# Loads, constants and one tile's projection moved across the phase borders of layer 0 in a two-layer latent-token backbone

## The chip, the cores and the metric

The kernel runs on one NeuronCore of a Trainium2 chip. The metric is the device time of one execution in microseconds (us), median of three runs. In the rows, PE is TensorE (PEld its weight loads), DVE VectorE, ACT ScalarE, POOL GpSimd, SP SyncE, which issues all DMAs of this kernel (SPq is its queue). PEclk is the clock granted to TensorE as a share of full speed.

## What is computed

Two layers over 256 context tokens and 2048 latent tokens of width 1024, in fp32. Layer 0 is the part that matters here. From normalized rows `h` one wide projection gives `u, v, ga, q, k, vv, gb`; two heads groups use it, and one output projection joins them:

```python
u, v, ga, q, k, vv, gb = _split(h @ w_in, AB_SIZES)
ya = chunk_gmlp(gelu(u), gelu(v), ln_g, ln_b, w_s, b_s) * silu(ga)   # group norm of v, then
                                   # u * (w_s @ v + b_s) in chunks of 128 tokens, 4 groups
yb = window_attention(q, k, vv, kc, vvc, sink) * silu(gb)            # +-128 tokens and context
y  = concatenate([ya, yb]) @ w_out
x  = x + gate * y
```

Layer 1 is a gated linear recurrence in both directions (`r, ig = sigmoid(z @ w + b)`, `a = exp(-8 * r * softplus(-lam))`, a scan per direction), followed by a last normalization. Its convolution weights, biases and `softplus(-lam)` are constants which the kernel prepares during layer 0.

## The kernel before

A tile is 128 tokens: 2 context and 16 latent tiles, `t` from 0 to 17, 9 pairs. fp32 products are made from two fp32r parts (high and low): each block is three matmuls, lines 91, 92 and 93 (`mm3`), with 128x512 results for a tile's projection on 512 columns, 8 blocks, 24 matmuls.

Layer 0 has three phases, each with its own pools of SBUF and PSUM. A pool of a later phase takes the memory that an earlier one gave back, and each of its tiles waits for the last users of the place.

**Attention** (to about 658 us). For every tile: normalized rows are transposed, split and spilled to DRAM (`h0s`), `q` and `k`, `vv` are projected, and scores (`pc`, `pl`), softmax, transposes (`ptp`), values (`po`, line 574) and the output (`os`) follow for units of two heads, some steps behind. The program merges these lists by fractions, and a scheduler orders each engine's instructions by priority and modelled readiness. Into attention fillers are put which need only `h`: `ga` of tiles 2 to 17 and, in its last three steps, a queue `tail_q` with `ga` of tiles 0 and 1 and the values `v` of the tiles in `V_TILES` (`pu`, written to `gv`). `TAIL` says how much of the queue each quarter step takes. Low-priority work (`FILL`) prepares layer 1's weights (`keep_halves`, `whl`, `kept`).

**Mixing** (to about 854 us; pools `a2b1`, `a2b2`). For each tile: rows are loaded (`load_h`, line 778, three buffers), `v` comes from `gv` or is projected (`pvv`), gelu and group norm give `vhl`, `u` is projected (`pu`), and per pair the 128x128 mixing (`sv`), the scale and bias and the transposes (`yatp`) give `ya`, written to `yas`. `consts()` is called after tile 0's values: it loads and transposes `w_s` (`wstp`), loads 92 rows of constants (`cr`), transposes them (`cvtp`) and computes the softplus. The sixth unit of weights for `u` is split at the beginning of the phase (ScalarE the high part, GpSimd the low parts).

**Gates and output** (pools `a3b1`, `a3b2`). `gate_b(pr)` loads the attention output of a pair (`ot`) and its rows (`hp3`, line 919, one buffer), projects the gate (`pg`, 96 matmuls of 128x256) and gives `ybT`; `out_a(t)` multiplies with `w_out` (`po`: blocks 0 to 3 with `yaT`, 4 to 7 with `ybT`, two halves, 48 matmuls).

Weights live in pools `wa` (3 buffers), `wb0` (2) and `wb` (1), used in turn. SyncE issues in order: a DMA that waits for its buffer holds all behind it.

Of the kernel before, what the change touches and what calls it, by code (L numbers as in the profile page):

```python
# [15 lines left out]
P = 128  # L16
D = 1024
KT = D // P
# [10 lines left out]
GA_FROM = 2  # L29
FILL = 400  # L30
WG_AT = (3, 5, 7, 9)
V_TILES = (3, 5, 7, 9, 11, 13, 15)
TAIL = (0, 4, 8, 12, 16, 20, 24, 28, 32, 38, 44, 50, 56)
U_AT = 5
T_PE = 14
BACK = 13
LAG = 4
MOD_AT = 8
# [4 lines left out]
def backbone_kernel(ctx: ExitStack, tc: tile.TileContext, a, out):  # L43
# [221 lines left out]
    with ExitStack() as c1:  # L265
# [375 lines left out]
        for i, (_, mm) in enumerate(tail):  # L641
            tail_q += mm
            if i + 2 < len(tail):
                tail_q.append(tail[i + 2][0])
            if i == U_AT:
                tail_q += wu_halves(wa, 4)
        n_tail = [len(tail_q) * f // TAIL[-1] for f in TAIL]

        def mod_bank():
# [70 lines left out]

    w_out0 = a["ab_w_out"][0]


    with ExitStack() as c2:
        b1 = c2.enter_context(tc.tile_pool(name="a2b1", bufs=1, reuse_waits="tile"))
# [2 lines left out]
        lng = bc_row(b1, a["a_ln_g"][0], "lng", 512)  # L728
        lnb = bc_row(b1, a["a_ln_b"][0], "lnb", 512)

        def consts():
            wsr = raws.tile([P, 4, P], F32, tag="raw", name="wsr")
            sp.dma_start(wsr, a["a_w_s"][0].rearrange("g p q -> p g q"))
            wsT = b1.tile([P, 2, 4, P], F32R, name="wsT")
            tp = bank([P, 4, P], "wstp", "t")
            for g in range(4):
                pe.transpose(tp[:, g], wsr[:, g], ident)
            split(wsT[:, 0], wsT[:, 1], tp)
            cr = raws.tile([92, P], F32, tag="raw", name="cr")
            r0 = 0  # L740
            for src in (a["c_conv_w"][0].rearrange("k (c p) -> (k c) p", p=P), a["c_conv_b"][0].rearrange("(c p) -> c p", p=P),
                        a["c_b_a"][0].rearrange("k (c p) -> (k c) p", p=P), a["c_b_i"][0].rearrange("k (c p) -> (k c) p", p=P),
                        a["c_lam"][0].rearrange("k (c p) -> (k c) p", p=P), a["a_b_s"][0]):
                n = src.shape[0]
                sp.dma_start(cr[r0:r0 + n], src)
                r0 += n
            tpc = bank([P, 92], "cvtp", "t")
            pe.transpose(tpc, cr, ident[0:92, 0:92])
            dve.tensor_copy(cv[:, 0:92], tpc)
            bs = cv[:, 88:92]  # L750

            def softplus_neg(pool_):
                t = [pool_.tile([P, 16], F32, name=f"spt{i}") for i in range(4)]
                dve.tensor_scalar(t[0], lam, -1.0, None, ALU.mult)
                dve.tensor_tensor(t[1], t[0], lam, ALU.min)
                act.activation(t[1], t[1], AF.Exp)
                dve.tensor_scalar(t[2], t[1], 2.0, None, ALU.add)
                dve.reciprocal(t[2], t[2])
                dve.tensor_tensor(t[1], t[1], t[2], ALU.mult)
                dve.tensor_tensor(t[2], t[1], t[1], ALU.mult)  # L760
                dve.memset(t[3], 2.0 / 19.0)
                for i in range(8, -1, -1):
                    dve.tensor_tensor(t[3], t[3], t[2], ALU.mult)
                    dve.tensor_scalar(t[3], t[3], 2.0 / (2 * i + 1), None, ALU.add)
                dve.tensor_tensor(t[3], t[3], t[1], ALU.mult)
                dve.tensor_scalar(t[0], t[0], 0.0, None, ALU.max)
                dve.tensor_tensor(sps[:, 0], t[0], t[3], ALU.add)
                dve.tensor_scalar(sps[:, 1], sps[:, 0], 4.0, None, ALU.mult)
                dve.tensor_scalar(sps[:, 2], sps[:, 0], -8.0, None, ALU.mult)

            softplus_neg(b1)
            return wsT, bs

        ubs, vhls, hps, ths = {}, {}, {}, {}

# [67 lines left out]
                act.activation(yT[:, x], tp, AF.Copy)  # L843
            sp.dma_start(yas[pr].rearrange("p x (g c) -> p x g c", c=P), yT)

        with tc.high_priority():
            load_h(0)
        load_h(1)
        wu = wus + [unit_w(wu_cols(5), act, (pool, pool))]
        part_g(0)  # L850
        wg, wo, halves = [], [], []
# [18 lines left out]
        for t in range(NT - 2):  # L870
            load_h(t + 2)
            if t:
                part_g(t)
            part_v(t)
            if t == 0:
                wsT, bs = consts()
            if t in WG_AT:
                halves.pop(0)()
            if t in WO1_AT:
                with tc.high_priority(offset=-FILL):  # L880
                    ahead.pop(0)()
            part_u(t)
            if t % 2 == 0 and t:
                pair_b(t // 2 - 1)
# [20 lines left out]
    with ExitStack() as c3:  # L905
# [7 lines left out]
        def gate_b(pr):  # L913
            ot = b2.tile([P, 2, 4, P], F32, tag="ot", name="ot")
            for x in range(2):
                sp.dma_start(ot[:, x], os_[2 * pr + x])
            hp = b1.tile([P, 2, 2, KT, P], F32R, tag="hp3", name="hp3")
            for x in range(2):
                sp.dma_start(hp[:, x].bitcast(F32), h0s[2 * pr + x])
            ybT = b2.tile([P, 2, 4, 2, P], F32R, tag="ybT", name="ybT")  # L920
            for half in range(2):
                pg = bank4([P, 2, 2, P], "pg")
                for cc in range(2):
                    for k in range(KT):
                        mm3(pg[:, cc], lambda hl: wg[half][:, hl, k, cc * P:(cc + 1) * P],
                            lambda hl: hp[:, :, hl, k], k == 0, k == KT - 1)
                sg = b2.tile([P, 2, 2, P], F32, tag="sg", name="sg")
                act.activation(sg, pg, AF.Silu)
                dve.tensor_tensor(sg, sg, ot[:, :, 2 * half:2 * half + 2].rearrange("p t c q -> p c t q"), ALU.mult)
                c = slice(2 * half, 2 * half + 2)  # L930
                split(ybT[:, 0, c], ybT[:, 1, c], sg)
            return ybT
# [54 lines left out]
        for pr in range(NPAIR):  # L987
# [4 lines left out]
            for x in range(2):  # L992
                if pr == NPAIR - 1 and x == 0:
                    op0 = next_w().tile([P, KT, 2, 2, P], F32R, tag="w", name="op0")
                    sp.dma_start(op0.bitcast(F32), h1s[0])
                    wx = [unit_w(w_in1[:, 0:U], act, (dve, dve))]
                if pr == NPAIR - 1 and x == 1:
                    ahead = []
                    for i in range(2, 2 + N_AHEAD):
                        ahead.append(raws.tile([P, 4, U], F32, tag="raw", name="raw"))  # L1000
                        unit, half = divmod(i, 2)
                        src = w_in1[512 * half:512 * half + 512, U * unit:U * (unit + 1)]
                        sp.dma_start(ahead[-1], src.rearrange("(k p) c -> p k c", p=P))
                f = out_a(2 * pr + x, yaT, ybT)
                if pend:
                    pend()
                pend = f
                for n in [1] if (pr, x) == (0, 0) else [pr + 2] if x else []:
                    if n < NPAIR:
                        gated.append(gate_b(n))  # L1010


    L = NPAIR
# [519 lines left out]
```

## Time and profile before

| | |
|---|---|
| median of 3 runs | 1976.6 us (1975.62 to 1977.08) |
| profiled execution | 1978.54 us |
| its span, first to last instruction | 1976.8 us |
| mean granted clock of TensorE | 0.982 |
| busy: PE, DVE, ACT, POOL | 1879.1, 1450.0, 1060.8, 564.7 us |
| moved by DMA | 371 MB, 188 GB/s on average |

All rows below are from that one execution, with times from the start of its span. A row of a timeline gives start, duration, engine, line, operation, what is written and read, how many, and in brackets the idle time of the engine before it and what ended it. A row of waits gives the engine, what it was about to run, whom it waited for, total us, times and the longest.

### The profile page before, as it was taken

What the parts mean: (1) busy time and instruction counts of PE and PEld (TensorE: products, weight loads), DVE (VectorE), ACT (ScalarE), POOL (GpSimd) and SP (SyncE); (2) the same over time, 40 slices, a digit from 0 to 9 for tenths busy, and PEclk for the clock granted to TensorE, in tenths of its full rate; (3) what the DMA queues carried; (4) which work ended last, traced back from release to release, by engine and by line L of the source; (5) the groups of instructions that cost most, each with busy time, mean ns of one, the idle gap of its engine ahead of it and who ended that gap; (6) DMA issues with size and microseconds to landing.
All of it is one profiled execution on the core that took longest, in us unless ns stands there. A gap on an engine that the chain in (4) does not pass through costs nothing. (4 is left out here: it accounts for less than half of the span.)

```text
span 1976.8 us, 28764 instructions
## 1 busy us (share of the span) xinstructions
PE 1879.1 (95%) x9919; PEld 1577.9 (80%) x9919; DVE 1450.0 (73%) x2943; ACT 1060.8 (54%) x1965; POOL 564.7 (29%) x769
## 2 busy tenths in 40 slices
PE   7999999999999799979999999999999999899898
PEld 3778878888888688868888887888888877687677
DVE  7888989786755787636777842498989656978873
ACT  6656656675745443324544551376656666666542
POOL 2755555564422211210000000144421221312211
PEclk8999999999999899989999999999999999999999
DMA  9355443552345689366565664334535736955643
GB/s 351 126 176 179 156 171 118 178 175 91 129 134 171 205 328 354 131 245 226 188 242 193 230 203 159 112 123 155 179 134 178 239 140 229 322 194 175 201 152 123
DMA packets 174398, 371.28 MB, mean 188 GB/s; under 512 B 18566, under 2 KB 72586, under 8 KB 166060
## 3 DMA queue, kind: packets, MB, share of 16 engines
q1 hardware_dynamic: 174252, 369.44, 53.6%
q8 instruction: 78, 1.28, 0.3%
q14 instruction: 68, 0.56, 0.1%
HBM read 242.22 MB, written 127.17 MB: 187 GB/s over the span
## 5 line engine op out<-in xcount | busy, mean ns | idle before, releaser
L91 PE MATMUL px<-op,w 128*128 128x512 f32 (+1 forms) x576 | 220.4, 383 | 10.1 <-DMA op<-h1s 9.9
L92 PE MATMUL px<-op,w 128*128 128x512 f32 (+1 forms) x576 | 218.4, 379 | 0.0
L93 PE MATMUL px<-op,w 128*128 128x512 f32 (+1 forms) x576 | 218.4, 379 | 0.0
L544 POOL TENSOR_SCALAR s<-s,ri 128x640 f32<-128x640 f32 (+2 forms) x144 | 133.9, 943 | 96.6 <-DVE ri L541 92.6
L536 ACT ACTIVATE s<-s,mn 128x641 f32<-128x641 f32 (+2 forms) x144 | 113.4, 788 | 65.9 <-DVE mn L518 58.8
L85 ACT ACTIVATE pT<-ptp 128x512 fp32r<-128x512 f32 (+1 forms) x192 | 99.6, 535 | 90.7 <-PE ptp L562 87.6
L88 DVE TENSOR_TENSOR zhl<-zf,zhl 128x512 fp32r<-128x512 f32 x72 | 57.3, 805 | 115.0 <-ACT zhl L85 114.8
L91 PEld LDWEIGHTS px<-op,w 128*128 128x128 f32 x576 | 109.0, 189 | 36.4 <-DMA op<-h1s 16.8
L574 PE MATMUL po<-pT,v 128*128 128x256 f32 x656 | 130.5, 297 | 6.8 <-DVE pT L88 4.4
L1127 POOL TENSOR_TENSOR ig<-ig,zf 128x512 f32<-128x512 f32 x72 | 104.9, 1462 | 102.0 <-ACT ig L1125 91.1
L88 DVE TENSOR_TENSOR pT<-ptp,pT 128x512 fp32r<-128x512 f32 (+1 forms) x192 | 114.3, 604 | 23.5 <-ACT pT L85 22.9
L93 PEld LDWEIGHTS px<-op,w 128*128 128x128 f32 x576 | 108.9, 189 | 20.4
L92 PEld LDWEIGHTS px<-op,w 128*128 128x128 f32 x576 | 109.1, 189 | 19.7
L1170 POOL COPY carry<-T 128x1 f32<-128x1 f32 x60 | 47.9, 802 | 259.1 <-DVE T L1168 256.8
L902 DVE STREAM_TRANSPOSE h1T<-hrow 32x256 f32<-32x256 f32 x224 | 97.7, 436 | 31.1 <-ACT hrow L954 28.1
L92 PE MATMUL px<-w,op 128*128 128x512 f32 x256 | 103.0, 402 | 14.9 <-DVE op L88 14.9
L574 PEld LDWEIGHTS po<-pT,v 128*128 128x128 f32 x656 | 98.9, 189 | 17.8 <-DVE pT L88 9.0
L164 POOL TENSOR_SCALAR ms<-ss 128x1 f32<-128x1 f32 x36 | 10.1, 280 | 353.0 <-ACT junk L162 346.0
L562 PE MATMUL ptp<-ident,s 128*128 128x128 f32 x656 | 104.7, 274 | 3.9 <-POOL s L544 2.1
L91 PE MATMUL px<-w,op 128*128 128x512 f32 x256 | 102.2, 399 | 4.0 <-DVE xt L1276 4.0
L93 PE MATMUL px<-w,op 128*128 128x512 f32 x256 | 102.3, 400 | 0.0
L518 DVE CUSTOM_DVE_ANT_0 s<-pl,mask,mn 128x384 f32<-128x384 f32 (+1 forms) x128 | 76.0, 594 | 32.8 <-PE pl L516 31.4
(279 smaller groups left out, 5804.4 us busy)
## 6 DMA issues: line engine op xcount, KB each, us to landing
hp<-h0s SPq DMA_DIRECT2D x45, 1024.0 KB
op<-h1s SPq DMA_DIRECT2D x56, 512.0 KB
mraw<-in_w_mod SPq DMA_DIRECT2D x48, 512.0 KB
h0s<-hT SPq DMA_DIRECT2D x18, 1024.0 KB
h1s<-h1hl SPq DMA_DIRECT2D x36, 512.0 KB
xt<-in_x SPq DMA_DIRECT2D x32, 512.0 KB
gs<-gs SPq DMA_DIRECT2D x64, 256.0 KB
raw<-in_ab_w_in SPq DMA_DIRECT2D x22, 512.0 KB
```

Of the source, the lines that this page charges most:

```text
L85: act.activation(hi, src, AF.Copy)
L88: (eng_lo or dve).tensor_tensor(lo, src, hi.bitcast(F32), ALU.subtract)
L91: pe.matmul(ps, lhsT=lhs(0), rhs=rhs(0), start=first, stop=False)
L92: pe.matmul(ps, lhsT=lhs(1), rhs=rhs(0), start=False, stop=False)
L93: pe.matmul(ps, lhsT=lhs(0), rhs=rhs(1), start=False, stop=last)
L518: dve.tensor_tensor_reduce(out=s[:, 1 + 2 * P:1 + 2 * P + n_l], in0=pl[:, 0:n_l], in1=mask[:, 2 * P + off:2 * P + off + n_l], scale=-1.0, ...
L536: act.activation(s[:, 0:nk], s[:, 0:nk], AF.Exp, scale=-1.0, bias=st["mn"][:, row, i:i + 1], accum_out=st["sm"][:, i:i + 1])
L544: pool.tensor_scalar(s[:, 1:nk], s[:, 1:nk], ri[:, i:i + 1], 0.0, ALU.mult, ALU.add)
L562: pe.transpose(tp[:, x, h], s_t[h][:, 1 + i * P:1 + (i + 1) * P], ident)
L574: pe.matmul(pos[t, g][:, 2 * P * e:2 * P * (e + 1)], lhsT=vl, rhs=pT[:, hl, x], start=i == 0 and hl == 0, stop=i == n - 1 and hl == 1)
L902: dve.transpose(out[o, :, s], src[s, :, o])
L1127: pool.tensor_tensor(res[1], res[1], zfs.pop((d, i, b)), ALU.mult)
```

## The change

- `load_hp01` loads the rows of tiles 0 and 1 into one buffer of `wb0`, from two thirds of the tail's queue on; mixing takes them from there and no longer calls `load_h` for them.
- Tile 1 joins `V_TILES`: its `v` is projected in the tail, and read back in mixing.
- `consts()` becomes `spatial()`, called after tile 1's values, and `columns()`, at low priority after tile 4's. The mixing's bias `bs` gets a tile and a load of its own, four elements per partition straight from DRAM, and `cr` has 88 rows.
- `hp3` moves to a pool `gaterows`, opened before mixing; pair 0's rows are loaded at tile 12 of mixing (as the program is written).

```diff
-V_TILES = (3, 5, 7, 9, 11, 13, 15)
+V_TILES = (3, 5, 7, 9, 11, 13, 15, 1)
...
+HP3_AT = 12
...
+        hp01 = []
+
+        def load_hp01():
+            hp01.append(wb0.tile([P, 2, 2, KT, P], F32R, tag="w", name="hp01"))
+            for t in range(2):
+                sp.dma_start(hp01[0][:, t].bitcast(F32), h0s[t])
+
+        tail_q.insert(len(tail_q) * 2 // 3, load_hp01)
         n_tail = [len(tail_q) * f // TAIL[-1] for f in TAIL]
...
+    mid = ctx.enter_context(ExitStack())
+    gaterows = mid.enter_context(tc.tile_pool(name="gaterows", bufs=1, reuse_waits="tile"))
+
+    def load_pair(pr):
+        hp = gaterows.tile([P, 2, 2, KT, P], F32R, tag="hp3", name="hp3")
+        for x in range(2):
+            sp.dma_start(hp[:, x].bitcast(F32), h0s[2 * pr + x])
+        return hp
...
-        def consts():
+        wsT = b1.tile([P, 2, 4, P], F32R, name="wsT")
+        bs = b1.tile([P, 4], F32, name="bs")
+        sp.dma_start(bs, a["a_b_s"][0].rearrange("g p -> p g"))
+
+        def spatial():
...
+        def columns():
+            cr = raws.tile([88, P], F32, tag="raw", name="cr")
...
-        with tc.high_priority():
-            load_h(0)
-        load_h(1)
+        for t in range(2):
+            hps[t] = hp01[0][:, t]
...
-            if t == 0:
-                wsT, bs = consts()
+            if t == 1:
+                spatial()
+            if t == 4:
+                with tc.high_priority(offset=-FILL):
+                    columns()
...
+            if t == HP3_AT:
+                hp3 = [load_pair(0)]
...
-            hp = b1.tile([P, 2, 2, KT, P], F32R, tag="hp3", name="hp3")
-            for x in range(2):
-                sp.dma_start(hp[:, x].bitcast(F32), h0s[2 * pr + x])
+            hp = hp3.pop() if hp3 else load_pair(pr)
```

What stands in a row on an engine is set by the scheduler. From attention to mixing, TensorE before (`po` ends attention, `pvv` is tile 0's first projection in mixing; the brackets name the semaphores waited for):

```order
L574 MATMUL po<-pT,v 128x256 [waits DVE_49]
L574 MATMUL po<-pT,v 128x256 x2
L737 MATMUL wstp<-ident,wsr 128x128 [waits DMAHW3_49,DVE_49]
L737 MATMUL wstp<-ident,wsr 128x128 x3
L748 MATMUL cvtp<-ident,cr 128x92 [waits DMAHW4_49,DMAHW5_49,DMAHW1_49,DMAHW6_49,DMAHW0_49,DMAHW7_49,DVE_49,PE_49]
L91 MATMUL pvv<-w,hp 128x512 [waits DMAHW5_49]
L92 MATMUL pvv<-w,hp 128x512
L93 MATMUL pvv<-w,hp 128x512
```

The same place of TensorE after the change (lines of the changed file, one higher here; `hp_8190` is the buffer filled by `load_hp01`):

```order
L575 MATMUL po<-pT,v 128x256 [waits DVE_49]
L575 MATMUL po<-pT,v 128x256 x2
L92 MATMUL pvv<-w,hp_8190 128x512
L93 MATMUL pvv<-w,hp_8190 128x512
L94 MATMUL pvv<-w,hp_8190 128x512
```

The transposes of `w_s` moved behind 37 matmuls of tile 0, those of the constants to the middle of mixing, and `pvv` has no wait. In the tail, 15 of tile 1's 24 matmuls stand in one block behind tile 15's and eight transposes, the other nine in four pieces among the following scores.

From mixing to the gates, TensorE before (`sv` and `yatp` of the last pair, then the output projection):

```order
L93 MATMUL sv<-vhl,wsT 128x256
L842 MATMUL yatp<-ident,ub 128x128 x2
L91 MATMUL sv<-vhl,wsT 128x256
L92 MATMUL sv<-vhl,wsT 128x256
L93 MATMUL sv<-vhl,wsT 128x256
L842 MATMUL yatp<-ident,ub 128x128 x6
L91 MATMUL po<-w,yaT_10356 128x512
L92 MATMUL po<-w,yaT_10356 128x512
```

The same place of TensorE after:

```order
L92 MATMUL pg<-hp_9662,w 128x256
L93 MATMUL pg<-hp_9662,w 128x256
L92 MATMUL sv<-vhl,wsT 128x256
L93 MATMUL sv<-vhl,wsT 128x256
L94 MATMUL sv<-vhl,wsT 128x256
L92 MATMUL sv<-vhl,wsT 128x256
L93 MATMUL sv<-vhl,wsT 128x256
L94 MATMUL sv<-vhl,wsT 128x256
L863 MATMUL yatp<-ident,ub 128x128 x2
L94 MATMUL pg<-hp_9662,w 128x256
```

Pair 0's gate, which stood behind 12 `po`, now lies around the last `sv` and `yatp`: 38 `pg` ahead of these `sv`, 20 behind, then six `yatp`, 38 `pg`, and the 24 `po` on `yaT` in one row.

SyncE's queue at the same place, before (`h0s_69` to `h0s_72` are the rows of tiles 0 to 3, `os_123` to `os_126` the attention output of the same):

```order
L844 DMA yas_149<-yaT 128x1024 [waits Activation_49]
L916 DMA ot<-os_123 128x512 [waits DVE_49,PE_49]
L916 DMA ot<-os_124 128x512 [waits DMAHW7_49]
L919 DMA hp_10242<-h0s_69 128x2048 [waits DMAHW0_49]
L919 DMA hp_10242<-h0s_70 128x2048 [waits DMAHW1_49]
```

and after:

```order
L865 DMA yas_149<-yaT 128x1024 [waits Activation_49]
L738 DMA hp_10458<-h0s_71 128x2048 [waits DMAHW5_49,PE_49]
L941 DMA ot<-os_123 128x512 [waits DMAHW6_49]
L941 DMA ot<-os_124 128x512 [waits DMAHW7_49]
L964 DMA xt<-in_ctx 128x1024 [waits DMAHW0_49]
L941 DMA ot<-os_125 128x512 [waits DMAHW1_49]
```

The rows of pair 0 went far up, to the beginning of mixing, and the first load for pair 1, which waits for TensorE, now stands ahead of pair 0's `ot`.

## Rows read from the trace of the kernel before

**Rows 1.** Page, busy time by engine: us, share of the span, instructions.
```profile
PE 1879.1 (95%) x9919; PEld 1577.9 (80%) x9919; DVE 1450.0 (73%) x2943; ACT 1060.8 (54%) x1965; POOL 564.7 (29%) x769
```
**Rows 2.** Timeline of TensorE, from attention to mixing: start, us, instruction.
```profile
656.91 0.62 PE L574 MATMUL po<-pT,v 128*128 128x256 f32 x3 [0.34 <-DVE pT L88]
...
666.02 0.80 PE L91 MATMUL pvv<-w,hp 128*128 128x512 f32 x1 [2.25 <-DMA hp<-h0s]
...
670.97 0.40 PE L91 MATMUL pvv<-w,hp 128*128 128x512 f32 x1
671.20 0.40 PE L92 MATMUL pvv<-w,hp 128*128 128x512 f32 x1
```
**Rows 3.** Windows at mixing's end: width, busy us by engine, PEclk, DMA share, GB/s.
```profile
848.30:869.00 20.70, 8.22 (x27) 5.90 (x27) 7.29 (x8) 4.47 (x7) 3.12 (x2) 0.66 0.87 320
869.00:872.00 3.00, 3.00 (x14) 3.00 (x15) 0.00 (x0) 0.00 (x0) 0.00 (x0) 0.51 1.04 401
```
**Rows 4.** TensorE's waits, 632 to 668 us: us in total, times, longest.
```profile
PE cvtp L748 <- issue: 3.8, 1, 3.8
PE pvv L91 <- DMA hp<-h0s: 2.2, 1, 2.2
...
PE wstp L737 <- DVE o L585: 1.4, 1, 1.4
```
**Rows 5.** TensorE's waits, 848 to 900 us.
```profile
PE pg L91 <- DMA hp<-h0s: 6.0, 1, 6.0
PE sv L91 <- DVE ub L837: 2.7, 1, 2.7
PE po L91 <- ACT yaT L85: 2.0, 1, 2.0
PE yatp L842 <- DVE ub L837: 1.4, 1, 1.4
PE po L92 <- DVE yaT L88: 0.5, 1, 0.5
```
**Rows 6.** SyncE's queue at mixing's beginning.
```profile
660.23 0.54 SPq L778 DMA_DIRECT2D hp<-h0s  x1
...
670.80 8.60 SPq L910 DMA_DIRECT2D mc<-mod  x4
```
**Rows 7.** SyncE's queue at mixing's end.
```profile
857.07 1.37 SPq L916 DMA_DIRECT2D ot<-os  x2
858.50 0.94 SPq L919 DMA_DIRECT2D hp<-h0s  x2
```
**Rows 8.** Timeline of TensorE, the first gate's first and two later matmuls.
```profile
868.94 0.55 PE L91 MATMUL pg<-hp,w 128*128 128x256 f32 x1 [5.96 <-DMA hp<-h0s]
...
873.08 0.28 PE L93 MATMUL pg<-hp,w 128*128 128x256 f32 x1
...
873.20 0.28 PE L91 MATMUL pg<-hp,w 128*128 128x256 f32 x1
```
**Rows 9.** Timeline of GpSimd: low parts of the sixth weight unit.
```profile
659.25 5.62 POOL L88 TENSOR_TENSOR w<-raw,w 128x1024 fp32r<-128x1024 f32 x2 [9.75 <-issue]
```
**Rows 10.** Windows, the first 128 us of mixing.
```profile
666.00:794.00 128.00, 127.98 (x595) 105.90 (x596) 99.43 (x304) 47.91 (x74) 20.52 (x28) 0.98 0.92 328
```
**Rows 11.** Timeline of ScalarE and VectorE behind the first gate.
```profile
876.26 1.28 ACT L928 ACT_TABLE_LOAD   x1 [18.69 <-PE pg L93]
...
878.19 0.69 DVE L929 TENSOR_TENSOR sg<-sg,ot 128x512 f32<-128x512 f32 x1 [19.36 <-ACT sg L928]
878.92 0.63 ACT L85 ACTIVATE ybT<-sg 128x512 fp32r<-128x512 f32 x1 [0.76 <-DVE sg L929]
```
**Rows 12.** Windows at attention's end.
```profile
634.00:648.00 14.00, 12.51 (x88) 10.69 (x88) 13.20 (x44) 11.68 (x28) 4.88 (x11) 1.00 0.33 108
648.00:657.50 9.50, 7.80 (x53) 6.40 (x52) 5.32 (x9) 4.53 (x8) 1.36 (x2) 1.00 0.12 28
```
**Rows 13.** SyncE's queue in the tail: loads for its tiles.
```profile
571.75 7.04 SPq L620 DMA_DIRECT2D hp<-h0s  x2
```

More of the change, by code (lines that the diff above doesn't have):

```diff
@@ L729, in backbone_kernel @@
         lnb = bc_row(b1, a["a_ln_b"][0], "lnb", 512)
-        def consts():
+        wsT = b1.tile([P, 2, 4, P], F32R, name="wsT")
+        bs = b1.tile([P, 4], F32, name="bs")
+        sp.dma_start(bs, a["a_b_s"][0].rearrange("g p -> p g"))
+        def spatial():
             wsr = raws.tile([P, 4, P], F32, tag="raw", name="wsr")
             sp.dma_start(wsr, a["a_w_s"][0].rearrange("g p q -> p g q"))
-            wsT = b1.tile([P, 2, 4, P], F32R, name="wsT")
             tp = bank([P, 4, P], "wstp", "t")
@@ L738, in consts @@
             split(wsT[:, 0], wsT[:, 1], tp)
-            cr = raws.tile([92, P], F32, tag="raw", name="cr")
+        def columns():
+            cr = raws.tile([88, P], F32, tag="raw", name="cr")
             r0 = 0
@@ L742, in consts @@
                         a["c_b_a"][0].rearrange("k (c p) -> (k c) p", p=P), a["c_b_i"][0].rearrange("k (c p) -> (k c) p", p=P),
-                        a["c_lam"][0].rearrange("k (c p) -> (k c) p", p=P), a["a_b_s"][0]):
+                        a["c_lam"][0].rearrange("k (c p) -> (k c) p", p=P)):
                 n = src.shape[0]
@@ L746, in consts @@
                 r0 += n
[L747 to L750, printed above, removed]
+            tpc = bank([P, 88], "cvtp", "t")
+            pe.transpose(tpc, cr, ident[0:88, 0:88])
+            dve.tensor_copy(cv[:, 0:88], tpc)
             def softplus_neg(pool_):
@@ L771, in consts @@
             softplus_neg(b1)
-            return wsT, bs
         ubs, vhls, hps, ths = {}, {}, {}, {}
@@ L1010, in backbone_kernel @@
                         gated.append(gate_b(n))
+    mid.close()
     L = NPAIR
```

## The prediction

> **What bounds the kernel now.** I read the table of engines first: TensorE is busy for 95% of the span [rows 1], so a change counts only where it takes matmuls off TensorE, or closes a hole in its row, or keeps its clock up. Next I read the windows of the whole span and looked for slices in which TensorE is neither busy nor at its full granted clock. Layer 0 has two such places, both at a change of phase, and the change touches both. Place A is the step from attention to mixing: the last attention matmul starts at 656.91 us and the first projection of mixing at 666.02 [rows 2]. Place B is the step from mixing to the gates and the output projection, 848.3 to 872 us [rows 3]. Then I read, for each place, TensorE's waits and what ended them: at A 1.4 + 3.8 + 2.2 = 7.4 us, the last of it for a DMA of normalized rows [rows 4]; at B 6.0 + 2.7 + 2.0 + 1.4 + 0.5 = 12.6 us, the largest again for rows by DMA [rows 5]. The waits of a chain are not one cause each: what ends last at A is the load that SyncE issues only at 660.23 [rows 6], at B the one issued at 858.50 [rows 7].
>
> The clock comes on top. At A twelve matmuls lie between those starting at 666.02 and 670.97, 0.41 us each, while the step right after is 0.23 us [rows 2]: the engine had stood nearly still for 8 us and runs at the lower level (1.2 GHz) before it is back at 2.4. That is 4.95 - 12 x 0.233 = 2.15 us lost. At B the stretch from 848.3 to 869 shows 27 instructions and 8.22 us busy at a mean clock of 0.66, and the next 3 us 14 matmuls at 0.51 [rows 3]. The first is six sv products, eight transposes and twelve po products, at full clock 6 x 0.117 + 8 x 0.12 + 12 x 0.233 = 4.5 us, with about 0.9 us of pipeline ends that stay; 2.8 us are lost. The second would take 14 x 0.117 = 1.6 us by the step at full clock [rows 8], so 1.3 us are lost. Together 4.1 us.
>
> **Place A, the first two tiles loaded a phase ahead.** The changed kernel keeps rows 0 and 1 in a buffer of the weight pool that is free since tile 1's projection in the tail, long before attention ends. TensorE's list then goes from the last po straight to tile 0's pvv, which waits for nothing; the transposes of the constants stand later in the stream. So the 7.4 us of waits and the 2.15 us of half clock go: -9.5 us. The five transposes are still done (0.6 us, in both kernels). What is next late: tile 0's second projection needs the sixth weight unit, whose low part GpSimd finishes at 659.25 + 5.62 = 664.87 [rows 9], 7.3 us after the last po ended at 657.5. TensorE reaches it after 36 products, 36 x 0.233 = 8.4 us, so it is 1 us early for all of it, and the first half, 4.5 us after, has 4 us. Tile 2's rows come after 72 products, 16.8 us; they are issued some 3 us after attention ends, and by the row of tile 0 (issued 660.23, used 666.02) land 5.8 us later. I take no wait; the bounds are 0 and 4 us (GpSimd late by one split, 2.8 us, and a bit of low clock).
>
> The softplus of the constants (some 25 small VectorE operations between 664 and 670 in the trace) and ScalarE's exponential move into mixing, where VectorE is busy 99 of 128 us and ScalarE 48 [rows 10]. The exponential needs its table loaded and then the other one again; a load shows 1.28 us [rows 11]. 2.6 us on an engine that idles 60% of the stretch, with three banks of PSUM between it and TensorE: 0, bound 1.5.
>
> The scale of the mixing, four values per partition, is now read element by element on SyncE instead of as four rows of a table. The nearest rows are the four small loads of mc, each of twice as many elements: 8.60 us of SyncE for the four [rows 6]. So this one costs between 0 and 2.2 us of SyncE, I say 1.1. Behind it in the queue stand the gates' rows and tile 2's, with 16.8 us to spare: 0. (The Trainium skill, "DMA: Bandwidth & Descriptors", section "Rules for kernel authors", advises against this form, since a last dimension that isn't contiguous becomes one descriptor per element. The mc rows agree. The sum is the same by it, because nothing here waits on that queue for so short a time.)
>
> **Tile 1's values in the tail.** 24 products of 0.233 us = 5.6 us leave mixing, where TensorE is busy 127.98 of 128 us [rows 10]: -5.6 in full. They enter the end of attention. There TensorE has room: 12.51 of 14 us and 7.80 of 9.5 us are busy [rows 12]. But the order puts 15 of the 24 in one block right after tile 15's values, at about 632.8, ahead of the next scores; VectorE, which is busy 13.2 of the next 14 us and so bounds that stretch [rows 12], gets its next scores 15 x 0.233 = 3.5 us later. It has about 1 us of work left over at that time, so 2.5 us of its time are lost; the other nine products fall between instructions that wait for VectorE anyway, and cost some 0.5. So the tail grows by 3.0 us, between 1.6 (VectorE with more left over) and 5.6 (all of it). Net -2.6 us, from 0 to -4.
>
> The two loads ahead (2 MB) wait only for the first half of tile 1's projection, the last reader of their buffer. They go out some 4 us ahead of the load for tile 5, which stands behind the end of that projection at 571.75 [rows 13]. 2 MB take 5 to 6 us at the rate of place A, so tile 5's load starts 1 to 2 us late. It has room for it: the next load in the row goes out 6.7 us later (two issues over 7.04 us), when tile 3's products are through and tile 5's begin, and one load of 1 MB takes under 5.8. I take 0, bound 2.
>
> **Place B, the first gates' rows loaded in mixing.** The first gate's 96 products (pg, 0.117 us each [rows 8], 11.2 us) no longer wait for a load behind mixing's last write, and the scheduler has put them between the last sv products and transposes: 38, then six sv and two transposes, 20, six transposes, 38, and only then the 24 po products on yaT. The waits for ub (2.7 and 1.4 us) and yaT (2.0 and 0.5) fall under 4.4, 2.3 and 4.4 us of pg; the load's 6.0 is gone. So the 12.6 + 4.1 us could all go: -16.7.
>
> What is late next is in SyncE's queue. The rows of pair 1 go into the one buffer that pair 0 has, so their load waits for the last pg; and in the new order this load stands **ahead of** the attention output of pair 0 (ot), which stood before the gates' rows before the change [rows 7]. Let the last pg end at E. SyncE takes about 0.5 us for the load and 0.7 for each half of ot [rows 7]. By the row of place A, 5.8 us from issue to use for 1 MB with neighbours, ot is there at about E + 6. Then come VectorE's product with the gate, 0.69 us, and ScalarE's split, 0.63 [rows 11]: E + 7.3, and VectorE's low part 0.7 later. TensorE has 24 po products on yaT to do, 5.6 us, and then waits: 1.7 + 0.6 = 2.3 us. A wait of that size is followed at A by twelve matmuls at the low clock, 2.15 us, and in 869 to 872 by 1.3. I take 4 us for wait and clock. The lower bound is 0 (ot is small and could pass with the first packets); the upper one is the slowest such load in the trace, issued 858.50 [rows 7] and used at 868.94 [rows 8], 10.4 us: 0.5 + 10.4 + 2 - 5.6 = 7, with the clock 9 us. Net at B: -12.7. (The Trainium skill, same page, section "Queues, rings and completion order", says that each DMA engine takes descriptors in the order of its ring. That speaks against the change here, since ot then waits for the whole of pair 1's first megabyte. The trace of before has ot ahead and can't show it; by the rule the lower bound of 0 falls away and the sum stays.)
>
> **The sum.** -9.5 - 2.6 - 12.7 = -24.8 us. The profiled execution took 1978.5 us: 1953.7. The median of the runs, 1976.6, is 1.9 us below it, and I keep that distance: 1952. After the second gate the order of every engine is as before, so the rest shifts as a whole.
>
> **The rivals.** First, ot comes in time and the tail hides tile 1: 4 + 1.4 us more, 1946 to 1948. For it: the queue is nearly empty then, as the 2 MB are gone from it. Against: the order puts ot behind a load that waits for TensorE. Second, ot comes as late as the slowest load: 5 us less gain, and with tile 1's values hidden not at all 1957 to 1960. Third, the change does not do at A what it says: the rows are there, but TensorE stops at the sixth weight unit, whose split waits for ScalarE and GpSimd behind attention's last work. If it ends 4 us late, with 2 us of low clock, 1958. Against it stand the 4 and 1 us of room above.
>
> Fourth, slower: the DMA engines become the bound of mixing. They are busy 0.92 of the 128 us after 666, at 328 GB/s [rows 10]. The same bytes (two tiles' rows leave, one pair's rows enter, 0.25 MB for tile 1's values) must now pass in about 128 - 2.2 - 5.6 = 120 us, a share of 0.98. If that is over what they can do, rows come late tile by tile, and each late tile costs a wait and low clock, 2.2 + 2.15 us [rows 2, 4]. Six such tiles eat the 24.8 us; eight, every second of the sixteen, give 1987. Against it: TensorE did not wait once in that stretch, three buffers of rows run ahead, and the loads of tiles 2 to 4 are now issued further ahead of their use.
>
> **How the numbers follow.** The forecast, 1948 to 1957 with 1952 as its value: 0.58. All hidden, down to 1946: 0.15. Second and third rival, 1957 to 1961: 0.19. The DMA engines partly in the way, so that less than 4 us is left: 0.04; wholly, slower: 0.04. Eight in ten lie between 1946 and 1962. A measurement of this kernel tells 0.2%, about 4 us, from no change. Faster by more: 0.92, within: 0.04, slower by more: 0.04.
>
> **What would show it.** At A: no wait of TensorE for rows, wstp or cvtp, pvv of tile 0 right behind the last po, clock 1.0 throughout. In the tail: the last po some 3 us later than 656.91. In mixing: no wait for rows, and its length from the first pvv to the last pu shorter by 5.6 + 2.2 us. At B: pg between the sv products at full clock, and one wait, of po on ybT, for an ot load. I am wrong if TensorE waits for the sixth unit or for rows in mixing, or if the tail grows by more than the 5.6 us it takes on.

## Result and profile after the change

The changed kernel takes 1954.9 us (median of four runs, 1952.7 to 1957.3) where the one before takes 1976.8 beside it: a ratio of 0.9893 (95% interval 0.988 to 0.9907), 22 us less. The forecast was 1952.0, from 1946 to 1962. The total came out three us above the forecast; the terms came out less well than the total. The profiled execution took 1957.3 us, its span is 1955.5 (before 1976.8), and TensorE is busy for 96% of it (95% in [rows 1]).

All waits of TensorE between 630 and 1140 us, after the change (us in total, times, longest):

```profile
PE po L92 <- ACT ybT L86: 5.2, 1, 5.2
PE ptp L563 <- DVE pT L89: 3.0, 2, 2.2
PE yatp L863 <- DVE ub L858: 0.9, 1, 0.9
PE po L575 <- DVE pT L89: 0.5, 2, 0.3
PE po L575 <- DVE o L586: 0.4, 1, 0.4
```

The 7.4 us of [rows 4] and the 12.6 of [rows 5] are gone. Two waits are new: 2.2 us of a transpose on a split of `pT`, in the tail, and 5.2 us of `po` on `ybT`, at place B.

**Place A** is closed. TensorE's row after (start, length, instruction), where [rows 2] has a hole from 657.5 to 666.0 and then twelve matmuls at the low clock:

```profile
662.60 0.62 PE L575 MATMUL po<-pT,v 128*128 128x256 f32 x3 [0.29 <-DVE pT L89]
663.06 0.39 PE L92 MATMUL pvv<-w,hp 128*128 128x512 f32 x1
663.29 0.40 PE L93 MATMUL pvv<-w,hp 128*128 128x512 f32 x1
663.53 0.40 PE L94 MATMUL pvv<-w,hp 128*128 128x512 f32 x1
```

The first projection follows the last `po` at once and every 0.23 us from the first one on. But the last `po` starts at 662.60 instead of 656.91: **the tail ends 5.7 us later**. What TensorE waits for there shows in the rows of VectorE and of SyncE's queue:

```profile
650.11 1.24 DVE L127 TENSOR_TENSOR raw<-raw,kgain 128x1024 f32<-128x1024 f32 x1 [0.39 <-DMA kgain<-mod]
651.27 0.68 DVE L89 TENSOR_TENSOR pT<-ptp,pT 128x512 fp32r<-128x512 f32 x1
```

```profile
641.34 0.34 SPq L631 DMA_DIRECT2D gv<-u  x1
641.73 0.43 SPq L755 DMA_DIRECT2D wsr<-in_a_w_s  x1
642.68 1.23 SPq L589 DMA_DIRECT2D os<-o  x2
643.95 0.60 SPq L123 DMA_DIRECT2D raw<-in_c_w_out  x1
644.59 0.49 SPq L126 DMA_DIRECT2D kgain<-mod  x1
```

The product with `kgain` belongs to the preparation of layer 1's weights, a piece of low priority. It stands in VectorE's row ahead of a split of `pT`; VectorE stands still for 0.39 us for its load and then works on it for 1.24 us, while the split is ready. The load was issued at 644.59, behind the write of tile 1's values (`gv`), which waits for their last product.

**Place B** in windows (length, busy us and count of TensorE, its weight loads, VectorE, ScalarE, GpSimd; then granted clock, DMA share, GB/s):

```profile
840.00:850.00 10.00, 10.00 (x88) 10.00 (x87) 7.41 (x8) 5.12 (x8) 2.56 (x2) 1.00 0.73 234
850.00:860.00 10.00, 9.12 (x55) 7.77 (x53) 0.00 (x0) 2.68 (x4) 0.00 (x0) 1.00 0.96 334
860.00:865.00 5.00, 0.68 (x2) 0.50 (x2) 2.00 (x4) 1.24 (x2) 0.00 (x0) 0.70 1.04 420
865.00:870.00 5.00, 5.00 (x16) 3.98 (x15) 0.60 (x1) 0.00 (x0) 0.00 (x0) 0.62 0.60 229
```

Up to 859 TensorE runs through at full clock, the gate's products between the `sv` products as foreseen. Then it waits, and the 16 instructions of the next window run at 0.62. The wait, in SyncE's queue, VectorE's row and TensorE's row:

```profile
853.64 0.32 SPq L738 DMA_DIRECT2D hp<-h0s  x1
854.02 0.90 SPq L941 DMA_DIRECT2D ot<-os  x2
```

```profile
862.91 1.30 DVE L952 TENSOR_TENSOR sg<-sg,ot 128x512 f32<-128x512 f32 x2 [14.65 <-DMA ot<-os]
```

```profile
864.32 1.22 PE L92 MATMUL po<-w,ybT 128*128 128x512 f32 x2 [5.19 <-ACT ybT L86]
```

`ot` goes out right behind pair 1's rows, as the prediction read from the order, but it comes 8.9 us after its issue, not 5.8.

### The profile page after: what moved, and what is told of

Its sections match the earlier page's. It is cut to its first block, busy times and chain, and to the rows that moved or that the text cites. A ratio compares the mean times of both kernels' runs of the same rounds, so it can differ in the third digit from the quotient of the medians.

```text
span 1955.5 us, 28765 instructions
## 1 busy us (share of the span) xinstructions
PE 1871.5 (96%) x9919; PEld 1573.9 (80%) x9919; DVE 1446.6 (74%) x2943; ACT 1063.6 (54%) x1968; POOL 567.7 (29%) x769
## 5 line engine op out<-in xcount | busy, mean ns | idle before, releaser
L563 PE MATMUL ptp<-ident,s 128*128 128x128 f32 x656 | 105.2, 276 | 5.6 <-DVE pT L89 3.5
L165 POOL TENSOR_SCALAR ms<-ss 128x1 f32<-128x1 f32 x36 | 10.9, 304 | 340.9 <-ACT junk L163 333.9
```

The lines of the kernel that those rows point to most:

```text
L563: pe.transpose(tp[:, x, h], s_t[h][:, 1 + i * P:1 + (i + 1) * P], ident)
```

## Experiments

The twelve kernels below were each timed in five rounds beside the kernel before. The ratio is from the timed runs; the four columns behind it, in us, are from the trace of one execution each. "Tail" runs from the first `pu` of the tail (551.6 us before the change) to the start of the last `po`; "gap" is from the end of the last `po` to the first `pvv`; "middle" from there to the first `px` of layer 1, "layer 1" from there to the end of the span.

| kernel | ratio to before (95%) | tail | gap | middle | layer 1 |
|---|---|---|---|---|---|
| before | 1 | 105.3 | 8.5 | 505.8 | 805.0 |
| changed | 0.9893 (0.9880-0.9907) | 111.3 | 0 | 490.7 | 801.7 |
| a1_values_in_mixing | 0.9921 (0.9908-0.9934) | 110.4 | 0 | 494.1 | 803.7 |
| a2_ot_early | 0.9865 (0.9851-0.9880) | 111.0 | 0 | 487.2 | 800.4 |
| a3_gate_rows_late | 0.9940 (0.9924-0.9955) | 111.3 | 0 | 500.5 | 798.7 |
| a4_keep_later | 0.9891 (0.9879-0.9904) | 111.5 | 0 | 489.6 | 801.6 |
| b1_tail_kept_clear | 0.9887 (0.9871-0.9903) | 108.3 | 0 | 491.1 | 800.5 |
| b2_clear_no_tile1 | 0.9901 (0.9887-0.9915) | 104.8 | 0 | 493.7 | 806.4 |
| b3_clear_ot_early | 0.9853 (0.9839-0.9867) | 108.4 | 0 | 483.7 | 799.0 |
| b4_rows_late | 0.9948 (0.9933-0.9963) | 111.0 | 9.3 | 491.3 | 800.6 |
| c1_before_three_loads | 1.0042 (1.0028-1.0057) | 105.2 | 8.1 | 508.8 | 805.7 |
| c2_best_five_loads | 0.9901 (0.9883-0.9919) | 108.6 | 0 | 491.4 | 803.9 |
| c3_best_two_loads | 0.9877 (0.9859-0.9895) | 108.2 | 0 | 489.3 | 801.2 |
| c4_constants_first | 0.9895 (0.9874-0.9916) | 111.9 | 0 | 490.7 | 801.4 |

Where the text gives us for a ratio, it is the ratio's difference times 1976.8.

### Tile 1 back in mixing

```
-V_TILES = (3, 5, 7, 9, 11, 13, 15, 1)
+V_TILES = (3, 5, 7, 9, 11, 13, 15)
```

> The changed kernel with one part undone: tile 1's values (24 products) are computed in mixing again. In the changed kernel the last po of attention starts at 662.60 us, 5.7 us later than before, which is as much as the 24 products take. Theory: tile 1's values fill no idle time in the tail, they lengthen it by all they cost. Then the last po comes back to about 657, mixing grows by 5.6 us, and the time is that of the changed kernel, 1955, within 2 us. By the prediction's price (tail +3.0, mixing -5.6) it is 2.6 us slower, 1957.5. Rival: the tail grew from something else in the change, the two loads ahead or the preparation of c_w_out that stands in VectorE's row there; then the last po stays near 661 and the time is 1959 to 1960.5.

Measured: 5.5 us slower than the changed kernel, and the tail 110.4, nearly as long without the 24 products as with them. The theory falls, and the rival holds (its time, 1959 to 1960.5, was a little low: the ratio gives 1961.2): something else lengthens this tail. ScalarE's and VectorE's rows show foreign pieces (work of a later phase), others than in the changed kernel, each with a wait for its load:

```profile
649.06 1.06 ACT L86 ACTIVATE w<-raw 128x1024 fp32r<-128x1024 f32 x1 [2.16 <-DMA raw<-in_ab_w_in]
```

```profile
657.70 1.22 DVE L127 TENSOR_TENSOR raw<-raw,kgain 128x1024 f32<-128x1024 f32 x1 [0.71 <-DMA kgain<-mod]
```

### The preparation of c_w_out begun later

```
-WO1_AT = (2, 4, 6, 8, 10, 11, 12, 13)
+WO1_AT = (7, 8, 9, 10, 11, 12, 13, 14)
```

> The changed kernel with the preparation of layer 1's c_w_out begun at tile 7 of mixing instead of tile 2, one piece per tile from there, which takes its first piece out of VectorE's row in the tail. In the changed kernel that piece makes VectorE wait 0.39 us for its row of gains and work 1.24 us, while the next split of pT is ready; TensorE waits 2.2 us and then runs at a mean clock of 0.83 for 10 us. Theory: that costs the tail 3 us. Then the last po starts near 659.5 and the time is 1952 (1950.5 to 1953.5). Rival: VectorE bounds the tail by its whole work and the products ahead of it, and the piece costs no more than its 1.2 us: the last po near 661.5 and the time 1953.5 to 1955, or later if the pieces are in the way at the end of mixing.

Measured: no difference (0.9891), tail 111.5. The piece with `kgain` is gone from the tail, and another has come in its place, a split of the gates' weights, in ScalarE's row:

```profile
648.28 1.06 ACT L86 ACTIVATE w<-raw 128x1024 fp32r<-128x1024 f32 x1 [1.06 <-DMA raw<-in_ab_w_in]
```

So taking one piece away tells nothing; whatever is next in line moves up. This called for a kernel that holds back all of them.

### A tail without foreign work, with tile 1 and without

A number is written by attention's last output, and the buffers into which mixing loads those weights are touched with it before their load:

```
+                if t == NT - 1 and g == 1:
+                    pool.tensor_copy(done, o2[0:1, 0, 0:1])
...
         raw = raws.tile([P, kh, n], F32, tag="raw", name="raw")
+        if held:
+            pool.tensor_copy(raw[0:1, 0, 0:1], done)
         sp.dma_start(raw, v[:, kh * h:kh * h + kh])
...
         for t in range(NT - 2):
+            held[:] = [1] if t < 7 else []
```

> The changed kernel with one thing added: the loads with which mixing prepares the gates' weights and layer 1's c_w_out wait, up to tile 6, for attention's last output, so that none of their splits stands in the rows of ScalarE and VectorE ahead of attention's last splits. In the changed kernel, with tile 1's values in mixing, and with c_w_out begun later, the tail is equally long (from the first pu to the last po 111.3, 110.4 and 111.5 us, against 105.3 before), and each time another piece of such work stands ahead of a split of pT and waits for its load (0.4 to 2.2 us). Theory: these pieces lengthen the tail, because the constants no longer hold two of the six buffers that they need. Then the distance falls to 106 to 108.5 and the time is 3 to 5 us below the changed kernel's (ratio to before 0.9868 to 0.9878). Rival: the tail is that long because of the 24 products and VectorE's own work; then the distance stays at 110 to 111 and the time at 0.989, or above it where the work put off is late in mixing.

> The same with tile 1's values in mixing again, which gives these 24 products their own price in a tail without foreign work. Theory: the distance from the first pu to the last po is that of before, 105.3 us (within 1), since nothing is left in the tail that was not there; the time is 0.5 to 4 us above the run with the products in the tail, as mixing gains 5.6 us and the tail loses 1.6 to 5 (the prediction said 3.0). Rival: something else in the change, the two loads ahead, lengthens the tail: the distance stays at 108 or more.

Measured: tails of 108.3 and 104.8 us. Without foreign work and without tile 1 the tail is that of before, so the two loads ahead cost it nothing; tile 1's 24 products cost 3.5 us of tail; foreign work costs the changed kernel another 3.0, by longer waits of TensorE (1.6 us more of them than in b1) and by 1.7 us lost at a lower clock, of which b1 has none. TensorE's waits in the tail of the first of the two are back to small ones:

```profile
PE po L581 <- DVE pT L91: 0.7, 2, 0.3
PE ptp L569 <- DVE pT L91: 0.6, 1, 0.6
```

In the timed runs the clear tail is worth 1.2 us of those 3.0, where 3 to 5 were expected, and the intervals overlap; the gain stands on the traces, not on the timed runs. Tile 1 in the tail is worth 2.8 us (0.9901 against 0.9887), with overlapping intervals too.

### Constants at tile 0 again

```
-            if t == 1:
+            if t == 0:
                 spatial()
-            if t == 4:
-                with tc.high_priority(offset=-FILL):
-                    columns()
+                columns()
```

> The changed kernel with one part undone: the constants (the transposes of the spatial weights and of layer 1's columns, with the softplus) are prepared at tile 0 again; rows 0 and 1 are loaded in the tail, as in the changed kernel. In the row of TensorE the transposes now stand behind the first 22 and 48 rows of tile 0's products, whose rows of x are there. Theory: place A's gain hangs on the rows, and moving the constants gives nothing of its own but the lengthening of the tail by foreign work: the gap between the last po and the first pvv stays at 0.5 us, the tail is 0 to 3 us shorter, and the time is the changed kernel's or up to 3 us less, a ratio of 0.9878 to 0.9895. Rival: the transposes wait for their loads behind attention, as at place A before (3.8 and 1.4 us, and 2 us of low clock), and the time is 3 to 7 us more, 0.991 to 0.993.

Measured: 0.9895, the gap closed, as the theory said; but the tail is 111.9, not shorter. The rival is right in half: a transpose (`cvtp`) waits 2.4 us for VectorE.

```profile
683.12 0.29 PE L771 MATMUL cvtp<-ident,cr 88*128 88x88 f32 x1 [2.44 <-DVE wsT L89]
```

So my reading in the expectation of b1, that foreign work enters because the constants no longer hold two buffers, is not the whole of it. Foreign pieces that wait or are late are there with the constants moved and tile 1 not (a1), with tile 1 moved and the constants not (this kernel), and with both moved but rows 0 and 1 not loaded ahead (b4, below). They are not there with none of the three (before). So none of the three is needed for it; a kernel with one of them alone was not run, and which of them suffices stays open.

### Rows of tiles 0 and 1 loaded late

```
-        tail_q.insert(len(tail_q) * 2 // 3, load_hp01)
...
-        for t in range(2):
-            hps[t] = hp01[0][:, t]
+        with tc.high_priority():
+            load_h(0)
+        load_h(1)
```

> The changed kernel with one part undone: rows 0 and 1 of mixing are loaded when mixing begins, as before; the constants stay in mixing, tile 1 in the tail. Theory: place A is worth the 8.5 us between the last po and the first pvv of before and the 2.15 us of half clock behind it, and all of it hangs on these rows; then the time is 9.5 to 10.6 us above the changed kernel's, a ratio of 0.994 to 0.9947. Rival: half of it belonged to the constants, whose loads and transposes no longer stand between; then TensorE waits 4 to 5 us less than before and the time is 4 to 6 us above, 0.9913 to 0.9923.

Measured: 0.9948, 10.9 us slower, just over the theory's upper end. The hole is back, with the low clock behind it (0.4 us a step instead of 0.23):

```profile
673.77 0.41 PE L770 MATMUL cvtp<-ident,cr 88*128 88x88 f32 x1 [7.13 <-DVE wsT L89]
673.89 0.77 PE L92 MATMUL pvv<-w,hp 128*128 128x512 f32 x1
674.47 0.63 PE L93 MATMUL pvv<-w,hp 128*128 128x512 f32 x1
```

Here the order has the transposes ahead of `pvv` again, and the last of the chain is named as a split of VectorE. By the completion events in the trace (sixteen for each DMA), tile 0's row has landed at 672.51, 1.3 us before the first `pvv`, so the last 1.3 us of this hole are the transposes'. With the rows there (c4) the same transposes do not keep `pvv` from starting. The rows carry place A.

### Gate rows late, and ot early

The first undoes the load of pair 0's gate rows ahead, by giving them a buffer of the gates' phase; the second adds a load of `ot` ahead.

```
-            if t == HP3_AT:
-                hp3 = [load_pair(0)]
...
-            hp = hp3.pop() if hp3 else load_pair(pr)
+            hp = b1.tile([P, 2, 2, KT, P], F32R, tag="hp3", name="hp3")
+            for x in range(2):
+                sp.dma_start(hp[:, x].bitcast(F32), h0s[2 * pr + x])
```

> The changed kernel with one part undone: the gate rows lie in a buffer of the gates' phase again, so the load of pair 0's waits for mixing's last write. Theory: place B is worth what the two traces show there, 10.4 us of the 18.0 by which layer 1's first products come earlier. Then TensorE waits some 12 us between the last sv products and the output projection again, and the time is 1965 (1963 to 1968; by the prediction's 12.7 us 1967.6). Rival: part of that gain is not this load's, since ot then stands ahead of pair 1's rows again and mixing has 2 MB less to move; then it is 1957 to 1961.

```
             if t == HP3_AT:
                 hp3 = [load_pair(0)]
+                ot0 = [load_ot(gaterows, 0)]
...
-            ot = b2.tile([P, 2, 4, P], F32, tag="ot", name="ot")
-            for x in range(2):
-                sp.dma_start(ot[:, x], os_[2 * pr + x])
+            ot = ot0.pop() if ot0 else load_ot(b2, pr)
```

> The changed kernel with one thing added: the attention output of pair 0 (ot, 0.5 MB) is loaded right behind pair 0's gate rows, in mixing, into a buffer of its own, instead of behind pair 1's rows. Theory: the 5.2 us in which po waits for ybT, and the 2.2 us that the 24 products after it lose at the lower clock, come from ot standing behind pair 1's rows. Then po does not wait, the stretch to the first pg of pair 1 shortens by 7.4 us, and the time is 1947.5 (1946 to 1949). Rival: something else is late next, pair 1's rows themselves or the rows of x, and 3 us or less is won: 1952 to 1955.

Measured: the gate rows are worth 9.3 us (0.9940), 9.8 in the middle of the trace, as the theory had it. With `ot` early the wait on `ybT` is gone and 5.5 us are won (0.9865), not 7.4: a wait of 2.0 us of `sv` on `vhl`, with 1.7 us lost at the lower clock behind it, has come in mixing.

```profile
PE sv L94 <- DVE vhl L89: 2.0, 1, 2.0
```

### Both additions

> Both additions together: no foreign work in the tail, and ot of pair 0 loaded in mixing. Loading ot early gave 5.5 us (ratio 0.9865 against 0.9893). Theory: the places are 200 us apart and the gains add up: 8.5 to 10.5 us below the changed kernel, a ratio of 0.984 to 0.985. Rival: the work put off from the tail meets the ot load and the gate rows in mixing, and less than 6 us is left: 0.9863 or more.

Measured: 0.9853 (1947.8 us beside 1976.5), 7.9 us below the changed kernel's ratio; a little under the theory's 8.5 to 10.5 and over the rival's 6. It is the fastest of all, faster than both given kernels, with intervals that touch at no point. The wait on `vhl` of a2 is not there, and at place B the order of pair 0's last `po` and pair 1's `pg` runs through at full clock, 0.23 us a step:

```profile
860.36 0.40 PE L94 MATMUL po<-w,ybT 128*128 128x512 f32 x1
860.59 0.39 PE L95 MATMUL po<-w,ybT 128*128 128x512 f32 x1
860.82 0.39 PE L96 MATMUL po<-w,ybT 128*128 128x512 f32 x1
861.35 0.35 PE L94 MATMUL pg<-hp,w 128*128 128x256 f32 x1
```

### Layer 1: the count of DMAs

Layer 1's code and order are the same in all kernels, and yet its trace was 3.3 us shorter after the change. Three kernels add a few loads of 16 numbers that nobody uses, at the beginning of mixing (three to the kernel before, five and two to the fastest):

```
+        spare = cvp.tile([1, 3, 16], F32, name="spare")
+        for i in range(3):
+            sp.dma_start(spare[:, i], a["c_lam"][0][0:1, 0:16])
```

> The kernel before, with three tiny loads (16 numbers each, never used) added at the beginning of mixing, nothing else. The changed kernel issues three DMAs more than the one before, and in every kernel the completions of the DMAs are counted on eight semaphores in turn; so layer 1, whose instructions are the same, waits on other semaphores. In the traces layer 1, from its first px to the end, takes 803.7 to 806.4 us in the three kernels with the old count and 798.7 to 801.7 in the seven with three more. Theory: the count makes this difference. Then layer 1 takes 798 to 802 us here and the time is 2 to 5 us below the kernel before's, a ratio of 0.9975 to 0.999 with some loss at the beginning of mixing. Rival: the difference is scatter between runs, or comes from tile 1's values; then layer 1 takes 803 to 806 and the ratio is 1.000.

> The kernel with the clear tail and the early ot (0.9853), with five such tiny loads at the beginning of mixing, so that the count stands where it stands before the change (eight more). Theory of the count: layer 1 takes 803.5 to 806.5 us instead of 799.0, and the time rises by 3 to 6 us, a ratio of 0.987 to 0.988. Rival, scatter: 799 to 802 us and 0.985 to 0.986.

> The same with two tiny loads, a count that none of the kernels so far had. Theory of the count: layer 1 takes some other time, between 797 and 807 us, and in the timed runs the ratio goes with it, 0.9005 being impossible and 0.9845 to 0.988 open. Rival, scatter: 799 to 802 us and 0.985 to 0.986.

(The 0.9005 in the last text is a slip and stands for nothing.) Measured: layer 1 takes 805.7, 803.9 and 801.2 us. The second would have fitted the theory of the count, though its ratio (0.9901) is outside either range; the first refutes it, since it has the changed kernel's count and the old kernel's time. The count is not the cause. Layer 1 took 803.7 to 806.4 us in the four kernels with tile 1 in mixing and 798.7 to 803.9 in the ten others; that may be chance or an effect of that move, and it stays open. For chance speaks the part ahead of the tail: its instructions are the same in all fourteen kernels on every engine, and the first `pu` of the tail still starts anywhere from 548.8 us (b2) to 555.9 (c4). One trace's 3.3 us in one part are well within that.

The loads were not free, though. Three cost the kernel before 0.4% (1.0042, 8.3 us), five cost the fastest 9.5 us; two cost it 4.7, with intervals that overlap. With five, mixing's row loads go out later, behind them, in c2 and without them in b3:

```profile
667.25 2.10 SPq L764 DMA_DIRECT2D spare<-in_c_lam  x5
672.98 0.81 SPq L816 DMA_DIRECT2D hp<-h0s  x2
```

```profile
665.11 1.11 SPq L813 DMA_DIRECT2D hp<-h0s  x2
```

That is 11.1 us after the start of the last `po` instead of 6.4. The issues themselves take only 0.22 to 0.28 us each; the 2.10 run from the first one's start to the last one's end and hold a wait. What takes the time is shown by the waits of SyncE's queue in c2:

```profile
SPq L861 <- DMA lng<-in_a_ln_g: 1.6, 1, 1.6
SPq L768 <- DMA kgain<-mod: 0.9, 1, 0.9
SPq L764 <- DMA raw<-in_c_w_out: 0.7, 1, 0.7
```

Eight semaphores are used in turn, so an issue waits until the DMA eight places ahead has landed. The load of `gl` ahead of the rows stands eight places behind `lng`, because the five loads fill the places between, and goes out at 672.28, when `lng` has landed.

And TensorE waits for rows in mixing, which it did in no other kernel that loads rows 0 and 1 ahead:

```profile
679.97 0.47 PE L94 MATMUL pvv<-w,hp 128*128 128x512 f32 x1 [0.60 <-DMA hp<-h0s]
693.18 0.39 PE L96 MATMUL sv<-vhl,wsT 128*128 128x256 f32 x1 [1.54 <-DVE vhl L91]
```

## Why the prediction came out as it did

I added up TensorE's idle time and its busy time times (1 - granted clock), window by window of 1 us, in the traces; the rows on products in mixing are what is left of the middle without these. Set against the prediction's terms, in us:

| step | predicted | measured |
|---|---|---|
| A: waits and low clock | -9.5 | -11.0 (gap 8.7, clock 2.3); undone +10.9 |
| tail: tile 1's products | +3.0 | +3.5 |
| tail: foreign work | not seen | +3.0 |
| mixing without the 24 products | -5.6 | -5.9 (b2 to b1), -5.0 (a1 to changed) |
| mixing: new wait, transposes of A done there | 0 | +1.6 |
| B: waits and low clock gone | -16.7 | -17.2 |
| B: wait on ot, with clock | +4 | +7.4 (5.2 and 2.2) |
| layer 1 | 0 | -3.3 |

The measured terms add up to -21.9, the spans differ by 21.3, against the -24.8 of the sum. (The chances of the bands up to 1961 add up to 0.92, which is more than the eight in ten given to the whole range.)

**Place A: right.** Rows there, no wait, full clock at once. What I feared did not come: TensorE never waited for the sixth weight unit (third rival), and the softplus in mixing cost it nothing that a wait shows. The load of `bs` takes 0.43 us of SyncE, where I bounded it by 0 and 2.2 and took 1.1:

```profile
667.01 0.43 SPq L751 DMA_DIRECT2D bs<-in_a_b_s  x1
```

(The Trainium skill, "DMA: Bandwidth & Descriptors", section "Rules for kernel authors", advises against this form. On SyncE this one load costs no more than its neighbours. The four `mc` loads, of the same form with twice as many elements, take 0.37, 4.23, 5.51 and 0.58 us there in the same trace, so the average of four that I scaled down was no price of one; why two of them take so long, and what the form costs the DMA engines, no run here shows.)

**Tail: the term right, the sum wrong.** The 24 products cost 3.5 us, near the 3.0 I took, and the two loads ahead nothing that the tail shows, although by the completion events their 2 MB took 10.2 us from the first issue and not 5 to 6, and tile 5's row landed 2.1 us later than before: the room that the prediction counted on was there. The step that failed is an omission: I priced what the change puts into the tail and did not ask what else the scheduler would put there. The order would have shown it, had I read ScalarE's and VectorE's rows up to the last split of `pT`; in the traces it is this: before the change the piece with `kgain` stands 31 instructions ahead of it, after it 14, with a split of weights two ahead of ScalarE's last. Before, that piece starts without a wait; where the load is issued late, it holds an engine with attention's splits behind it. "The tail grows by more than the 5.6 us it takes on" was written as a sign of being wrong, and 5.7 is over that line, by this cause and not by the products.

**Mixing: no wait for rows, as forecast, but a smaller gain.** From the first `pvv` to the last `pu` it is 176.5 us instead of 181.1: 4.6 shorter, where the prediction's sign said 5.6 + 2.2. A wait of 0.9 us of `yatp` on `ub` and the 0.6 us of the transposes now done there are part of the difference; some 1.6 us stay unexplained. TensorE waited for no row, though the DMA engines were busy all the time, so the fourth rival is refuted for this kernel:

```profile
700.00:750.00 50.00, 48.99 (x234) 39.68 (x233) 43.99 (x131) 21.82 (x34) 10.26 (x13) 1.00 1.01 369
```

How near it was shows in c2: 4.7 us of delay in SyncE's queue, and rows come late.

**Place B: the mechanism right, the size wrong.** The one wait that was named came, at the place named, for the reason named; a2 and b3 take it away by loading `ot` ahead. The mis-sized term is the time from issue to use of `ot`: taken as 5.8 us from place A's row, measured 8.9, with the DMA engines at 0.96 to 1.04 from 850 to 865. The steps behind it (product and split, 1.4 us) and the 5.6 us of products that cover it were right, and so 2.3 us of wait became 5.2; the low clock behind it cost 2.2 and not 1.7. My upper bound, 9 us, held. I should have taken the row nearer in place, the loads issued from 858.50 on in [rows 7]: they too had mixing's last writes and the next phase's loads beside them, while A's had nearly idle DMA engines ahead (a share of 0.12 in [rows 12]). The 10.4 us to their use [rows 8] are those of two loads of 1 MB; by the completion events the first of them landed after 7.8 us, and pair 1's first row after the change also took 7.8. (The Trainium skill, same page, section "Queues, rings and completion order", has each DMA engine take its ring's descriptors in order. The trace agrees: the sixteen completions of pair 1's row come from 858.16 to 861.44, those of the first half of `ot` from 858.80 to 862.11 and of the second from 859.88 to 862.78. The lower bound of 0 was indeed void.)

**After the second gate** I said that the rest shifts as a whole. It shifted by 18.0 us up to layer 1's first `px`, and layer 1 was 3.3 us shorter still. Without that the span would have come out some 7 us above the sum instead of 3.5, so part of the good total is luck: it is owed to something the prediction did not contain and the runs did not explain.

## What to carry to other kernels

When a change makes room in buffers or in a queue, look at what a scheduler moves into it: read the in-order row of each engine up to the last instruction of the phase, and ask of every piece that belongs to the next phase whether its load was issued early enough. A load that waits for a buffer must not stand ahead of one that waits for nothing and is needed sooner; moving the small one ahead of the border gave another 5.5 us here (a2). Take a transfer's time from a row with the same neighbours in the queue, not from one with the same size.

## What the runs showed of the hardware

A load of 64 bytes keeps SyncE for 0.22 to 0.44 us (the ten in c1, c2 and c3), a load of a quarter of a megabyte for 0.43 (`wsr` above). In a stretch in which the DMA engines are busy throughout, five of the small ones cost 9.5 us and three of them 8.3, several times their issue time. In c2 part of the way is shown above: a DMA issued behind them has to wait for one that was issued ahead of them. The rest of that cost, and c1's, stays open.

After the wait of 5.2 us at place B the granted clock stood at 0.50 from 862.0 to 868.8, and 2.2 us were lost. The wait of 2.2 us in the tail, with shorter ones around it, was followed by 1.7 us lost between 650 and 660, the wait of 2.0 us in a2 by 1.7, the waits under 1 us in mixing by none. The length of the wait alone does not tell: the 2.4 us before `cvtp` in c4 came amid full rows of products, and the granted clock stayed at 1.00 from 668 to 700.
